# Scan tables of a hybrid decoder trunk: encoding table on GpSimd, direct table by one matmul a group

## Chip, core and metric

One core of a Trainium2 chip runs the whole program in one launch. The metric is device time in microseconds (us); lower is better. Engines are named as in the profile: PE (matmuls; PEld its weight loads), DVE (vector), ACT (scalar), POOL (GpSimd), SP (which here only issues DMAs).

## What is computed

The reference is a two-layer trunk over 256 positions of width 2048. Layer 0 runs a Mamba-2 scan and attention side by side; layer 1 is an S5 mixer: 128 groups of 16 channels, each driving a 64-dimensional diagonal complex state. Both layers end in a layer norm. The change is about small tables for layer 1 that depend on parameters alone and are made while layer 0 runs. Cut to what matters:

```python
def reference(x, ...):
    h = ssd_moba_mixer(x, ...)                 # layer 0
    x = layer_norm(ALPHA * x + h, ...)
    h = s5_mixer(x, ...)                       # layer 1
    return layer_norm(ALPHA * x + h, ...)

def s5_mixer(x, w_in, ...):
    u, gate = jnp.split(x @ w_in, 2, axis=-1)
    y = gelu(s5_ssm(u, ...))
    ga, gb = jnp.split(y @ w_glu, 2, axis=-1)
    return (ga * sigmoid(gb) * silu(gate)) @ w_out

def s5_ssm(u, ...):
    lam_bar = jnp.exp(lam * dt)                                 # per group, 64 complex
    b_bar = ((lam_bar - 1.0) / lam)[..., None] * (b_re + 1j * b_im)
    # h[t] = lam_bar * h[t-1] + b_bar @ u[t];  y[t] = Re(c @ h[t]) + d * u[t]
```

## The kernel before

**Big products.** Nearly all time is in products with weights in fp32, which are split in two parts: a weight unit of 128x1024 is loaded by SP into `raw` (L227), ACT copies it into `wh` in the reduced format fp32r (L230), DVE forms the rest `wl` (L232), and PE multiplies with both (L276, L282, L285). `raw`, `wh` and `wl` have four buffers each. A unit is 12 to 16 matmuls; PE goes through 433 units in a fixed order, and the splits are written three units ahead of their use (`split_to`).

**Small work between units.** Everything else is cut into jobs. After each unit `pump` runs one or more of `jobs` (due soon) and of `back` (spread evenly up to a goal). The framework then orders the instructions of each engine by a simulation of the time they take; `tc.issue_after(x)` keeps what stands under it behind x. At run time each engine, SP's and POOL's queues too, goes through its own list in that order and waits at the head of it for semaphores. A tile of a pool with `bufs=1` can be filled again only when all readers of its last content are done.

**Scan tables.** Layer 1 takes four positions at a time, so each of the 16 blocks of 8 groups needs in DRAM (`wb[b]`, 128x1792): an encoding table (512 columns, four inputs to the state), a decoding table (512), a direct table (256, inputs to outputs inside the four) and phasors (512). The jobs for a block are in `block_jobs` and `phasors`; block 0 begins near 390 us, they end near 790 us, and `ssm` of layer 1 loads `wb[b]` from 870 us on.
- `bars` loads `bc` on SP (L722) and weighs B; `efs` and `fcs` form the encoding table `et` and the decoding table `ob` on DVE (L748 to L762).
- `pes`, once for two blocks: eight transposes on PE turn `et` (L398), ACT copies them into `ob` (L772), which ACT stores; 16 matmuls of `et` with `cv` give the first column of the direct table (L779).
- `mts`: three matmuls with shift matrices (L789) give the other columns, three ACT copies place them (L793).
- `phasors`: on POOL alone, L698 to L711. Four sums of the rotary embedding (L938) in each of the four head groups of the attention stand on POOL as well.

Of the kernel before, what the change touches and what calls it, by code (L numbers as in the profile page):

```python
# [16 lines left out]
P = 128  # L17
# [19 lines left out]
SLOT = np.array([[8 * (q // 4) + 4 * (q % 2) + 2 * ((q // 2 % 2) ^ h) + q // 2 % 2 for q in range(64)] for h in range(2)])  # L37
GORDER = [16 * h + p + 8 * i for h in range(8) for p in range(8) for i in range(2)]
# [13 lines left out]
NCONST = _fields(CONST, [("ident", 128), ("causal", 256), ("tril", 128), ("shift", 384),  # L52
# [5 lines left out]
def _constants():  # L58
# [39 lines left out]
def _layout(inp):  # L98
# [66 lines left out]
def trunk(tc, io, out):  # L165
# [8 lines left out]
    with ExitStack() as top:  # L174
# [33 lines left out]
        keep = [None, range(0)]  # L208

        def split_to(i):  # L210
            while nsplit[0] <= min(i, len(units) - 1):
# [15 lines left out]
                nc.sync.dma_start(raw.rearrange("p k n -> p (k n)"), units[n])  # L227
# [185 lines left out]
        wb = [dram.tile([P, 1792], F32, name=f"wb{b}") for b in range(16)]  # L413
        rho = cst.tile([P, 64], F32, name="rho")
# [8 lines left out]
        with ExitStack() as l0:  # L423
# [168 lines left out]
            lap = pp.tile([P, 2, 64, 4], F32, name="lap")  # L592
# [5 lines left out]
            def trig_jobs():  # L598
# [38 lines left out]
            def table_jobs():  # L637
                em, ex, th, lr = dtl[:, 0:128], ta[:, 0, 0:128], ta[:, 1, 0:128], ta[:, 2, 0:128]
                sn, sh, co, t0 = (tb[:, i, 0:128] for i in range(4))
                re, im = nre[:, 0:128], nim[:, 0:128]  # L640
                li = sh
                wr, wi = wri[:, 0, :], wri[:, 1, :]
# [14 lines left out]
                def reals():  # L657
                    V.tensor_tensor(wr, em, re, op=OP.mult)
                    V.tensor_tensor(th, li, im, op=OP.mult)
                    V.tensor_tensor(wr, wr, th, op=OP.add)  # L660
                    V.tensor_tensor(wr, wr, t0, op=OP.mult)

                def imags():
                    V.tensor_tensor(wi, li, re, op=OP.mult)
                    V.tensor_tensor(th, em, im, op=OP.mult)
                    V.tensor_tensor(wi, wi, th, op=OP.subtract)
                    V.scalar_tensor_tensor(wi, wi, sgn, t0, op0=OP.mult, op1=OP.mult)
                    V.tensor_copy(lam[:, 0, :, 0], lr)
                    V.tensor_copy(lam[:, 1, :, 0], li)

                def power(w, n, k, a, b):
                    def go():
                        tp, tq = t0[:, 0:n], th[:, 0:n]
                        ar, ai = w[:, 0, :, a], w[:, 1, :, a]
                        br, bi = w[:, 0, :, b], w[:, 1, :, b]
                        V.tensor_tensor(tp, ar, br, op=OP.mult)
                        V.tensor_tensor(tq, ai, bi, op=OP.mult)
                        V.tensor_tensor(w[:, 0, :, k], tp, tq, op=OP.subtract)
                        V.tensor_tensor(tp, ar, bi, op=OP.mult)
                        V.tensor_tensor(tq, ai, br, op=OP.mult)  # L680
# [753 lines left out]
```

## Time and profile before

| | us |
|---|---|
| median of 3 runs (lowest, highest) | 1336.08 (1334.17, 1336.17) |
| profiled execution, its time | 1333.94 |
| its span (first to last instruction) | 1332.2 |
| PE busy, DVE busy, ACT busy, POOL busy | 1316.2, 1006.2, 697.2, 388.1 |
| mean granted clock of PE | 0.995 |

How to read the lines: a group's line names the line of the code, engine, operation, output<-inputs with shapes, count, then busy time and mean ns, then idle time of the engine before them and what ended it. A timeline line is start, length, engine, line, names, count. A line by stretch has for PE, PEld, DVE, ACT and POOL the busy us with the instruction count, then the granted clock (1.00 is full), the DMA engines' share and GB/s. A line of waits is: who waited <- for what, total us, times, longest. Records of an fp32 matmul come in two, so 16 matmuls are 32 records.

### The profile page before, as it was taken

What the parts mean: (1) busy time and instruction counts of PE and PEld (TensorE: products, weight loads), DVE (VectorE), ACT (ScalarE), POOL (GpSimd) and SP (SyncE); (2) the same over time, 40 slices, a digit from 0 to 9 for tenths busy, and PEclk for the clock granted to TensorE, in tenths of its full rate; (3) what the DMA queues carried; (4) which work ended last, traced back from release to release, by engine and by line L of the source; (5) the groups of instructions that cost most, each with busy time, mean ns of one, the idle gap of its engine ahead of it and who ended that gap; (6) DMA issues with size and microseconds to landing.
All of it is one profiled execution on the core that took longest, in us unless ns stands there. A gap on an engine that the chain in (4) does not pass through costs nothing.

```text
span 1332.2 us, 21933 instructions
## 1 busy us (share of the span) xinstructions
PE 1316.2 (99%) x8240; PEld 1115.5 (84%) x8240; DVE 1006.2 (76%) x1642; ACT 697.2 (52%) x952; POOL 388.1 (29%) x650
## 2 busy tenths in 40 slices
PE   9999999999999999999999999899999999999996
PEld 8888888878888888888888888888888888888885
DVE  5879847897798888889788766749899845555565
ACT  5667669964644544554653434334345544444441
POOL 0050000123028547738887400013343100000001
PEclk9999999999999999999999999999999999999998
DMA  8555565555546657556756668397988665555662
GB/s 314 193 172 181 190 251 195 171 171 176 174 158 238 208 187 249 202 190 221 262 193 227 235 235 309 121 311 254 307 288 311 208 218 189 187 192 187 253 211 81
DMA packets 81915, 287.04 MB, mean 215 GB/s; under 512 B 9984, under 2 KB 12672, under 8 KB 81296
## 3 DMA queue, kind: packets, MB, share of 16 engines
q1 hardware_dynamic: 69264, 243.51, 53.5%
q0 software_dynamic: 7360, 30.45, 6.8%
q10 hardware_dynamic: 5184, 11.67, 2.4%
q8 instruction: 65, 1.06, 0.3%
q14 instruction: 42, 0.34, 0.1%
HBM read 264.58 MB, written 21.00 MB: 214 GB/s over the span
## 4 chain that ended last, share of the span: by engine, by line
PE 98%; DVE 1%; ACT 0%; POOL 0%; issue 0%; POOLq 0%
PE main L276 46%; PE main L282 27%; PE main L285 14%; PE main L328 2%; PE aux L398 1%; PE aux L282 1%; PE aux L871 1%; PE aux L779 1%; PE enc L1223 1%; PE aux L409 1%; PE aux L285 1%; PE dec L1268 1%; PE aux L958 1%; PE aux L990 1%; PE dec L1264 0%; PE aux L789 0%
## 5 line engine op out<-in xcount | busy, mean ns | idle before, releaser
L232 DVE TENSOR_TENSOR wl<-raw,wh 128x1024 fp32r<-128x1024 f32 x431 | 536.6, 1248 | 276.3 <-ACT wh L230 271.1
L230 ACT ACTIVATE wh<-raw 128x1024 fp32r<-128x1024 f32 x431 | 455.3, 1059 | 525.7 <-PE main L276 268.5
L282 PE MATMUL main<-AB,wh 128*128 128x512 f32 x1344 | 479.1, 400 | 0.0
L285 PE MATMUL main<-AB,wl 128*128 128x256 f32 x1344 | 378.5, 282 | 0.0
L276 PE MATMUL main<-wh,AB 128*128 128x512 f32 x1024 | 322.1, 392 | 0.0
L282 PEld LDWEIGHTS main<-AB,wh 128*128 128x128 f32 x1344 | 252.4, 188 | 60.6 <-issue 1.8
L285 PEld LDWEIGHTS main<-AB,wl 128*128 128x128 f32 x1344 | 253.8, 189 | 1.5 <-issue 0.8
L276 PE MATMUL main<-wh,CF 128*128 128x512 f32 x768 | 241.2, 392 | 0.0
L276 PEld LDWEIGHTS main<-wh,AB 128*128 128x128 f32 x1024 | 192.0, 188 | 40.3 <-issue 0.6
L276 PE MATMUL main<-wl,AB 128*128 128x512 f32 x512 | 199.9, 390 | 0.0
L276 PEld LDWEIGHTS main<-wh,CF 128*128 128x128 f32 x768 | 144.0, 188 | 30.5
L276 PE MATMUL main<-wl,CF 128*128 128x512 f32 x384 | 149.8, 390 | 0.0
L706 POOL TENSOR_TENSOR c<-c 128x8 f32<-128x8 f32 (+2 forms) x192 | 105.7, 569 | 30.2 <-DMA wb<-c 22.6
L276 PEld LDWEIGHTS main<-wl,AB 128*128 128x128 f32 x512 | 96.2, 188 | 19.3
L276 PEld LDWEIGHTS main<-wl,CF 128*128 128x128 f32 x384 | 72.1, 188 | 14.7
L938 POOL TENSOR_TENSOR a<-a,b 64x512 f32<-64x512 f32 x16 | 34.7, 2171 | 145.8 <-DVE a L937 115.7
L880 POOL TENSOR_TENSOR ssq<-ssq,c 128x256 f32<-128x256 f32 x16 | 21.4, 1337 | 191.2 <-ACT c L878 190.6
L282 PE MATMUL main<-CF,wh 128*128 128x512 f32 x192 | 68.3, 399 | 0.0
L708 POOL TENSOR_TENSOR c<-c,c 128x4 f32<-128x4 f32 (+2 forms) x96 | 54.9, 572 | 7.5
L285 PE MATMUL main<-CF,wl 128*128 128x256 f32 x192 | 54.0, 281 | 0.0
L709 POOL TENSOR_TENSOR c<-c,c 128x4 f32<-128x4 f32 (+2 forms) x96 | 47.0, 489 | 0.0
L1379 POOL DMA_DIRECT2D AB<-in_lnr x1 | 0.6, 554 | 157.4 <-issue 157.4
(282 smaller groups left out, 1431.9 us busy)
## 6 DMA issues: line engine op xcount, KB each, us to landing
raw<-in_wi SPq DMA_DIRECT2D x271, 512.0 KB, 3.8
raw<-in_wo SPq DMA_DIRECT2D x96, 512.0 KB, 3.8
raw<-in_wglu SPq DMA_DIRECT2D x64, 512.0 KB, 3.3
wt<-wb POOLq DMA_DIRECT2D x16, 896.0 KB, 7.5
wb<-ob ACTq DMA_DIRECT2D x16, 512.0 KB, 5.4
bc<-in_s5bc SPq DMA_DIRECT2D x16, 256.0 KB, 3.3
a<-cumd SPq DMA_DIRECT2D x8, 512.0 KB, 6.6
wb<-c POOLq DMA_DIRECT2D x16, 256.0 KB, 3.2
```

The lines of the kernel that those rows point to most:

```text
L230: high = A.activation(wh, raw, AF.Copy)
L232: splits[n] = (high, V.tensor_tensor(wl, raw, wh.bitcast(F32), op=OP.subtract))
L276: T.matmul(ps[o], l[:, k, sl], r[:, j, :], start=start and i == 0, stop=stop and i == 2)
L282: T.matmul(ps[o].rearrange("p (a n) -> p a n", a=2), wh[:, j, sl], x2[:, :, k, :], start=start, stop=False, skip_group_check=True)
L285: T.matmul(ps[o][:, 0:S], wl[:, j, sl], x2[:, 0, k, :], start=False, stop=stop, skip_group_check=True)
L328: T.matmul(pv[o // 2][:, o % 2, :], l[:, j, sl], r[:, k, :], start=first and i == 0 and o % 2 == 0, stop=end and i == 2 and o % 2 == 1, sk ...
L398: end = T.transpose(dst[:, i * P : i * P + P], s, ident)
L706: G.tensor_tensor(p[:, :, :, 0:m], cs[:, :, :, 1 : m + 1], cs[:, i, :, n : n + 1].unsqueeze(1).to_broadcast([P, 2, 4, m]), op=OP.mult)
L708: G.tensor_tensor(cs[:, 0, :, n + 1 : n + 1 + m], p0[:, 0, :, 0:m], p1[:, 1, :, 0:m], op=OP.subtract)
L709: G.tensor_tensor(cs[:, 1, :, n + 1 : n + 1 + m], p0[:, 1, :, 0:m], p1[:, 0, :, 0:m], op=OP.add)
L880: G.tensor_tensor(ssq, ssq, jk[:, f, :], op=OP.add)
L938: turns.append(G.tensor_tensor(q[0:64], q[0:64], tm, op=OP.add))
```

## The change

1. The encoding table is made already turned, with the inputs on partitions, so that no transpose is needed. `loads` gets two more tiles per block on SP: `bt` (B, 128x512) and `lt` (two DMAs, weights times powers of lam_bar, from a DRAM tile `qd` that new table jobs `qpower` fill). `etable` makes the table with four operations on POOL and stores it from POOL; the decoding table is stored from ACT.
2. The decoding side `ft` is made on DVE in the layout of the direct table's operands (`fcs`), and `bb` repeats the weighed B four times (`wides`). `pes` then is one matmul with 64 moving columns for each of the 16 groups of two blocks, which gives all four columns of the direct table at once, unmasked.
3. `mts` places and masks them: one ACT copy with a mask as scale and three DVE operations on shifted views of PSUM, in place of the shift matmuls.
4. `loads` is kept behind the last `raw` load written so far, and `etable` behind the last rotary sum (`turns[-1]`), as `phasors` was. `bt`, `lt` and `te` have one buffer, `et`, `bb` and `ft` two.

```diff
-                nc.sync.dma_start(raw.rearrange("p k n -> p (k n)"), units[n])
+                lastraw[0] = nc.sync.dma_start(raw.rearrange("p k n -> p (k n)"), units[n])
...
+                def qpower(i):
+                    def go():
+                        times(q(i), [m[:, 128:192] for m in (wr, wi)] if i == 3 else q(i + 1), [m[:, 128:192] for m in (lr, li)], 64)
+                        if i % 2 == 0:
+                            nc.gpsimd.dma_start(qd[i : i + 2].rearrange("s p x -> p s x"), tb[:, i, :].rearrange("p (s x) -> p s x", s=2))
+                    return go
...
                 def bars():
+                    with tc.issue_after(lastraw[0].ins):
+                        loads()
+                    wides()
+
+                def loads():
                     bc = h["bc"] = pp.tile([P, 4, 8, 16], F32, tag="bc", name=nm("bc"))
                     nc.sync.dma_start(bc.rearrange("p a g m -> p (a g m)"), io["s5bc"][b].rearrange("p a g m -> p (a g m)"))
...
+                    bt = h["bt"] = pp.tile([P, 2, 4, 64], F32, tag="bt", name=nm("bt"))
+                    nc.sync.dma_start(bt.rearrange("p r a n -> p (r a n)"), io["s5bt"][b])
+                    lt = h["lt"] = pp.tile([P, 4, 2, 64], F32, tag="lt", name=nm("lt"))
+                    for i in range(2):
+                        src = qd[:, 64 * i + 4 * b : 64 * i + 4 * b + 4, :].rearrange("s a x -> s (a x)")
+                        nc.sync.dma_start(lt[64 * i : 64 * i + 64].rearrange("p a r n -> p (a r n)"),
+                                          src.unsqueeze(0).to_broadcast([16, 4, 512]))
+
+                def wides():
+                    bc = h["bc"]
+                    bb = h["bb"] = pp.tile([P, 8, 16, 4], F32, tag="bb", bufs=2, name=nm("bb"))
+                    tm = pp.tile([P, 2, 8, 16], F32, tag="tm", name=nm("tm"))
+                    wr, wi = (wri[:, i, gs].unsqueeze(2).to_broadcast([P, 8, 16]) for i in range(2))
+                    V.tensor_tensor(tm[:, 0], bc[:, 0], wr, op=OP.mult)
+                    V.tensor_tensor(tm[:, 1], bc[:, 1], wi, op=OP.mult)
+                    t0, t1 = (tm[:, i].unsqueeze(3).to_broadcast([P, 8, 16, 4]) for i in range(2))
+                    V.tensor_tensor(bb, t0, t1, op=OP.add)
 
                 def fcs():
                     bc = h["bc"]
...
+                    ft = h["ft"] = pp.tile([P, 8, 16, 4], F32, tag="ft", bufs=2, name=nm("ft"))
+                    tm = pp.tile([P, 8, 16, 3], F32, tag="tm", name=nm("tm"))
+                    lr, li = (lam[:, i, gs, :].unsqueeze(2).to_broadcast([P, 8, 16, 3]) for i in range(2))
+                    ca, cb = (bc[:, i].unsqueeze(3).to_broadcast([P, 8, 16, 3]) for i in (2, 3))
+                    V.tensor_copy(ft[:, :, :, 0], bc[:, 2])
+                    V.tensor_tensor(ft[:, :, :, 1:4], ca, lr, op=OP.mult)
+                    V.tensor_tensor(tm, cb, li, op=OP.mult)
+                    V.tensor_tensor(ft[:, :, :, 1:4], ft[:, :, :, 1:4], tm, op=OP.add)
+
+                def ets():
+                    with tc.issue_after(turns[-1].ins):
+                        etable()
+
+                def etable():
+                    bt, lt = h["bt"], h["lt"]
+                    et = pp.tile([P, 4, 2, 64], F32, tag="et", bufs=2, name=nm("et"))
+                    te = pp.tile([P, 4, 2, 64], F32, tag="te", name=nm("te"))
+                    for r, dst in enumerate((et, te)):
+                        G.tensor_tensor(dst, lt, bt[:, r].unsqueeze(2).to_broadcast([P, 4, 2, 64]), op=OP.mult)
+                    G.tensor_tensor(et[:, :, 0], et[:, :, 0], te[:, :, 1], op=OP.subtract)
+                    G.tensor_tensor(et[:, :, 1], et[:, :, 1], te[:, :, 0], op=OP.add)
+                    nc.gpsimd.dma_start(wb[b][:, 0:512], et.rearrange("p a r n -> p (a r n)"))
+                    fv = h["ft"].rearrange("p (h q) m t -> p h (q m t)", h=2)
                     for r in range(2):
...
+                        dst = wb[b][:, 512 + 256 * r : 768 + 256 * r].rearrange("(h n) x -> n h x", h=2)
+                        nc.scalar.dma_start(dst, fv[64 * r : 64 * r + 64])
 
                 def pes():
...
+                    pk = hk["pk"] = aux()
+                    for n, d in enumerate((pend.pop(), h)):
+                        for q in range(4):
+                            for at in range(2):
+                                i = q // 2
+                                a = 2 * (q % 2) + (i ^ at)
+                                T.matmul(pk[64 * at : 64 * at + 64, 256 * n + 64 * a : 256 * n + 64 * a + 64],
+                                         d["bb"][:, 4 * at + q].rearrange("p m s -> p (m s)"),
+                                         d["ft"][:, 4 * at + q].rearrange("p m t -> p (m t)"), start=True, stop=True)
+
+                def mts():
+                    pk = hk["pk"].rearrange("p (a m t) -> p a m t", m=16, t=4)
                     dc = PR("s5d")[:, 4 * b - 4 : 4 * b + 4].unsqueeze(2).to_broadcast([P, 8, 16])
...
+                    V.tensor_tensor(dd, C("kmask").unsqueeze(1).to_broadcast([P, 8, 16]), dc, op=OP.mult)
+                    V.tensor_tensor(pk[:, :, :, 0], pk[:, :, :, 0], dd, op=OP.add)
+                    sm = C("smask")
+                    A.activation(om.rearrange("p a m t -> p (a m t)"), hk["pk"], AF.Copy, scale=sm[:, 0:1])
+                    for t in range(1, 4):
+                        V.scalar_tensor_tensor(om[:, :, :, t:], pk[:, :, :, : 4 - t], sm[:, t : t + 1], om[:, :, :, t:],
+                                               op0=OP.mult, op1=OP.add)
```

The changed code moves lines: weight loads on SP are L225 (before L227), weight matmuls L274 (L276), the phasor work L709 to L722 (L698 to L711), the rotary sums L956 (L938).

On PE, at the first pair of blocks, before: transposes of the two blocks' `et`, the direct matmuls, and, 20 weight matmuls later, the shift matmuls.

```order
L276 MATMUL main_4081<-wh_4084,AB_75 128x512
L398 MATMUL aux_4184<-consts,et_3874 128x128 x4
L398 MATMUL aux_4191<-consts,et_4109 128x128 x4
L779 MATMUL aux_4182<-cv_3809,et_3874 64x16 x8
L779 MATMUL aux_4182<-cv_4071,et_4109 64x16 x8
L276 MATMUL main_4080<-wh_4121,AB_75 128x512
...
L789 MATMUL aux_4252<-kt_4183,consts 128x128 x3
```

At the same place after:

```order
L274 MATMUL main_4092<-wh_4043,AB_75 128x512
L792 MATMUL aux_4147<-ft_3827,bb_3800 64x64 x8
L792 MATMUL aux_4147<-ft_4063,bb_4036 64x64 x8
L274 MATMUL main_4091<-wh_4071,AB_75 128x512
L274 MATMUL main_4091<-wl_4073,AB_75 128x512
```

Transposes and shifts are gone, and 16 matmuls of 64 columns stand where 16 of 16 columns stood.

On SP, at block 13 before: among the weight loads `raw` stands one load of `bc`.

```order
L227 DMA raw_7569<-in_wo 128x1024
L227 DMA raw_7599<-in_wo 128x1024
L722 DMA bc_7587<-in_s5bc 128x512
L227 DMA raw_7617<-in_wo 128x1024
L227 DMA raw_7645<-in_wo 128x1024
```

At block 13 after:

```order
L225 DMA raw_7350<-in_wo 128x1024
L225 DMA raw_7400<-in_wo 128x1024
L737 DMA bc_7418<-in_s5bc 128x512
L739 DMA bt_7420<-in_s5bt 128x512
L743 DMA lt_7422<-qd 64x1x512 x2
L225 DMA raw_7430<-in_wo 128x1024
L225 DMA raw_7454<-in_wo 128x1024
```

Behind `bc` stand the loads of `bt` and `lt`, and the next weight loads stand behind them; in the list of waits `bt` waits for POOL. This place is two weight loads earlier in the list than before.

On POOL, before, from the end of block 12's phasors (`wb_88` is block 12's part of DRAM, `wb_89` block 13's): nothing but phasors.

```order
L711 DMA wb_88<-c_1197_7519 128x512
L698 MEMSET c_1245_7807 128x4
L699 MEMSET c_1245_7807 128x4
L701 COPY c_1245_7807<-phi 128x4 x2
L706 TENSOR_TENSOR c_1246_7808<-c_1245_7807 128x8
```

After, block 12's encoding work (`et_7305`, which reads block 12's `bt_7226` and `lt_7228`) inside the phasors of block 13:

```order
L722 DMA wb_88<-c_1179_7368 128x512
L709 MEMSET c_1224_7634 128x4
...
L719 TENSOR_TENSOR c_1224_7634<-c_1225_7635,c_1226_7636 128x4x4
L776 TENSOR_TENSOR et_7305<-lt_7228,bt_7226 128x512
L776 TENSOR_TENSOR te_7306<-lt_7228,bt_7226 128x512
L720 TENSOR_TENSOR c_1224_7634<-c_1225_7635,c_1226_7636 128x4x4
L777 TENSOR_TENSOR et_7305<-et_7305,te_7306 128x4x64
L778 TENSOR_TENSOR et_7305<-et_7305,te_7306 128x4x64
...
L779 DMA wb_88<-et_7305 128x512
```

After the last rotary sum POOL's list is: phasors of block 8 (encoding of 9 inside), of 9, of 10 (encoding of 10 inside), of 11 (11 inside), of 12, of 13 (12 inside), of 14, of 15 (13 inside), then the encoding of 14 and 15. So the phasors, which wait for no load, run up to two blocks ahead of the encoding work, which waits for SP's loads.

More of the change, by code (lines that the diff above doesn't have):

```diff
@@ L37 @@
 SLOT = np.array([[8 * (q // 4) + 4 * (q % 2) + 2 * ((q // 2 % 2) ^ h) + q // 2 % 2 for q in range(64)] for h in range(2)])
+DUP = np.concatenate([SLOT[:, 4 * b : 4 * b + 4].reshape(-1) for b in range(16)])
 GORDER = [16 * h + p + 8 * i for h in range(8) for p in range(8) for i in range(2)]
@@ L671, in power @@
-                def power(w, n, k, a, b):
-                    def go():
[L673 to L680, printed above, removed]
-                        V.tensor_tensor(w[:, 1, :, k], tp, tq, op=OP.add)
-                    return go
@@ L684, in table_jobs, with weights @@
-                return [parts, norms, reals, imags] + [power(w, n, k, a, b) for w, n, top in ((lam, 128, 3), (lap, 64, 4))
-                                                       for k, a, b in ((1, 0, 0), (2, 1, 0), (3, 1, 1)) if k < top]
+                    V.tensor_tensor(ex, ex, th, op=OP.add)
+                    V.tensor_tensor(th, li, re, op=OP.mult)
+                    V.tensor_tensor(em, em, im, op=OP.mult)
+                def weights():
+                    V.tensor_tensor(th, th, em, op=OP.subtract)
+                    V.tensor_tensor(wr, ex, t0, op=OP.mult)
+                    V.tensor_tensor(wi, th, t0, op=OP.mult)
+                    V.tensor_scalar(wri[:, 0, :], wr[:, 0:128], nsg, None, op0=OP.mult)
+                    V.tensor_scalar(wri[:, 1, :], wi[:, 0:128], -1.0, None, op0=OP.mult)
+                    V.tensor_copy(lam[:, 0, :, 0], lr[:, 0:128])
+                    V.tensor_copy(lam[:, 1, :, 0], li[:, 0:128])
@@ new lines, in times, with power @@
+                def times(out, a, b, n):
+                    tp, tq = t0[:, 0:n], th[:, 0:n]
+                    V.tensor_tensor(tp, a[0], b[0], op=OP.mult)
+                    V.tensor_tensor(tq, a[1], b[1], op=OP.mult)
+                    V.tensor_tensor(out[0], tp, tq, op=OP.subtract)
+                    V.tensor_tensor(tp, a[0], b[1], op=OP.mult)
+                    V.tensor_tensor(tq, a[1], b[0], op=OP.mult)
+                    V.tensor_tensor(out[1], tp, tq, op=OP.add)
+                def power(k, a, b):
+                    def go():
+                        times(*([lam[:, i, :, n] for i in range(2)] for n in (k, a, b)), 128)
+                    return go
@@ new lines, in signed, with q @@
+                def signed():
+                    V.tensor_scalar(lam[:, 1], lam[:, 1], sgn, None, op0=OP.mult)
+                def q(i):
+                    return [tb[:, 2 * (i // 2), 128 * (i % 2) + 64 * r : 128 * (i % 2) + 64 * r + 64] for r in range(2)]
+                def qpower(i):
[4 more added lines that the diff above has]
+                    return go
@@ L687, in trunk @@
+                return [parts, norms, parts2, weights, power(1, 0, 0), power(2, 1, 0), signed] + [qpower(i) for i in (3, 2, 1, 0)]
             turns = []
```

134 lines of the change are left out of this document (32 added, 102 removed).

## The prediction

> **What bounds the kernel now.** I read the page's busy row and chain first, then busy time by stretch, then PE's timeline in the stage that the change touches, last the queues of POOL and SP there.
>
> ```profile
> span 1332.2 us, 21933 instructions
> PE 1316.2 (99%) x8240; PEld 1115.5 (84%) x8240; DVE 1006.2 (76%) x1642; ACT 697.2 (52%) x952; POOL 388.1 (29%) x650
> ...
> PE 98%; DVE 1%; ACT 0%; POOL 0%; issue 0%; POOLq 0%
> ```
>
> PE is busy for 99% of the span and is 98% of the chain. So an instruction less on PE is time won, as long as its weights keep coming. The stage with the tables (about 385 to 790 us) in its last third, and the one place where PE stood still:
>
> ```profile
> 617.00:757.00 140.00, 140.00 (x762) 117.73 (x761) 112.66 (x216) 69.56 (x97) 112.74 (x233) 1.00 0.68 232
> 840.00:860.00 20.00, 16.47 (x134) 15.45 (x132) 15.14 (x26) 5.54 (x10) 0.00 (x0) 0.91 0.15 53
> L232 DVE TENSOR_TENSOR wl<-raw,wh 128x1024 fp32r<-128x1024 f32 x45 | 56.8, 1266 | 26.6 <-ACT wh L230 26.4
> L232 DVE TENSOR_TENSOR wl<-raw,wh 128x1024 fp32r<-128x1024 f32 x65 | 79.7, 1226 | 79.6 <-ACT wh L230 78.9
> ```
>
> From 617 to 757 us PE never waits, while DVE (112.7 of 140, 80%) and POOL (112.7) are also nearly full. The third row is DVE's weight split in that stretch, the fourth the same from 1100 to 1280 us, where POOL is idle.
>
> **PE's part of the change.**
>
> ```profile
> 411.88 0.39 PE L276 MATMUL main<-wl,AB 128*128 128x512 f32 x1
> 412.11 0.39 PE L276 MATMUL main<-wh,AB 128*128 128x512 f32 x1
> 412.34 1.03 PE L398 MATMUL aux<-consts,et 128*128 128x128 f32 x8
> 413.30 1.11 PE L779 MATMUL aux<-cv,et 128*64 128x16 f32 x32
> 414.34 0.50 PE L276 MATMUL main<-wh,AB 128*128 128x512 f32 x1
> 414.68 0.39 PE L276 MATMUL main<-wl,AB 128*128 128x512 f32 x1
> ...
> 419.93 0.83 PE L789 MATMUL aux<-kt,consts 128*128 128x128 f32 x6
> 420.51 0.48 PE L276 MATMUL main<-wh,AB 128*128 128x512 f32 x1
> ...
> 226.90 1.52 PE L871 MATMUL aux<-b,CF 128*64 128x256 f32 x16
> 228.35 0.50 PE L282 MATMUL main<-AB,wh 128*128 128x512 f32 x1
> ```
>
> Starts count, not durations: weight matmuls start 0.23 us apart. Transposes and direct matmuls hold PE from 412.34 to 414.34, and the matmul behind them takes 0.34 instead of 0.23: 2.11 us. The shifts hold it for 0.58 (419.93 to 420.51) and about 0.1 behind: 0.68. A pair of blocks costs 2.79, eight pairs 22.3 us.
>
> After, a pair costs 32 records of 128 rows by 64 weight columns and 64 moving columns. From below, L779 has the same weight loads and 16 moving columns: 413.30 to 414.34, 1.04 us. The moving columns are priced by L871, also in two column halves: 16 records, eight with 256 and eight with 128 columns, 3072 in all, take 1.45 us, 0.47 ns a column; 2048 columns are 0.97 us. L871 loads its weights underneath, so I take the larger, 1.04, and 0.11 behind it: 1.15. From above the two add up: 2.12. PE's gain is 1.64 a pair (at least 0.67), **13.1 us** over eight pairs (at least 5.4).
>
> **DVE, ACT, DMA.** From 617 to 757 us:
>
> ```profile
> L748 DVE TENSOR_TENSOR et<-bb,lam 128x128 f32<-128x128 f32 x18 | 7.3, 440 | 0.0
> L749 DVE TENSOR_TENSOR tm<-bb,lam 128x128 f32<-128x128 f32 x18 | 7.1, 433 | 0.0
> L762 DVE TENSOR_TENSOR ob<-ob,tm 128x256 f32<-128x256 f32 x10 | 4.6, 460 | 0.2
> L735 DVE TENSOR_SCALAR cv<-bc,consts 128x128 f32<-128x128 f32 x6 | 3.2, 534 | 0.0
> L750 DVE TENSOR_TENSOR et<-et,tm 128x384 f32<-128x384 f32 x5 | 3.1, 611 | 0.0
> ```
>
> A block today: six strided products at 0.44, six of 128x256 at 0.46, one 128x384 at 0.61, eight small ones near 0.4 and half of a pair's three: some 9.8 us. After: three of 128x384 at 0.61, one 128x512 near 0.7, three small ones, half of a pair's five: 4.9. That takes 4.9 of a block's 26 us (below) off DVE: 80% becomes some 62%. ACT makes one copy a pair instead of five. The table jobs grow by nine operations and by half in width near 100 to 160 us, where PE never waits either. I cost all of this at nothing on PE's path: the cover is the splits' lead over PE (worked out below), and if that were gone, splits would come late there. The new loads bring 512 KB a block to SP's queue, one weight unit more in some eight, with DMA at 0.68.
>
> **POOL's and SP's part.** Call the phasor work of a block P (L698 to L711) and the new encoding work E: two multiplies of 128x512, two sums of 128x256, a DMA issue.
>
> ```profile
> 613.49 4.27 POOL L938 TENSOR_TENSOR a<-a,b 64x512 f32<-64x512 f32 x1 [4.33 <-DVE a L937]
> ...
> L722 SPq DMA_DIRECT2D bc<-in_s5bc x15: 327/328/382, 394.9 to 763.7; - x15
> ...
> L698 POOL MEMSET c<- x8: 124/126/182, 617.7 to 738.4; 128x4 f32 x8
> ...
> L711 POOL DMA_DIRECT2D wb<-c x8: 587/587/627, 635.0 to 756.4; - x8
> ...
>   POOL c L706: 17.3, 7
> ...
> L938 POOL TENSOR_TENSOR a<-a,b x16: 1263/1781/6302, 274.3 to 613.5; 64x512 f32<-64x512 f32 x16
> ...
> L880 POOL TENSOR_TENSOR ssq<-ssq,c x16: 733/1193/4335, 223.9 to 322.9; 128x256 f32<-128x256 f32 x16
> ```
>
> A block has 26.3 us (SP's loads of bc: 368.8 over 14). After the last rope sum (613.5) eight P run back to back from 617.7 to 757.0: 17.4 us each, 2.5 of it waiting for its own store (17.3 over 7). POOL is slower the busier DVE is: the same L938 takes 1263 to 1781 ns at the median. With DVE at 62% I take P = 15.7, a tenth off, nearer to the upper row because the splits stay; bounds 17.4 (no relief) and 13.1 (14.9 x 1263/1781 + 2.5: as if no DVE were beside it). E: multiply 1.9 (1.26 to 2.2), sum 1.1 (0.73 to 1.3), issue 0.59: **6.6 us** (4.6 to 7.6).
>
> Nobody on PE waits for P. E is different: the tiles bt and lt have one buffer, so SP may issue block b+1's load of bt only when E of block b has multiplied, and weight loads stand behind it on SP. The order above puts E of block 12 behind P of blocks 8 to 12 and 0.4 of 13, and E of block 13 another 2.2 P later.
>
> ```profile
> SPq L227 <- DVE wl L232: 235.5, 89, 5.8
> ACT wh L230 <- PE main L276: 268.5, 167, 3.3
> ...
> 700.82 12.71 SPq L227 DMA_DIRECT2D raw<-in_wo  x5
> 713.75 0.33 SPq L722 DMA_DIRECT2D bc<-in_s5bc  x1
> 715.58 16.88 SPq L227 DMA_DIRECT2D raw<-in_wo  x7
> 733.15 0.33 SPq L722 DMA_DIRECT2D bc<-in_s5bc  x1
> 735.17 2.41 SPq L227 DMA_DIRECT2D raw<-in_wo  x2
> ...
> L230 ACT ACTIVATE wh<-raw 128x1024 fp32r<-128x1024 f32 x431 | 455.3, 1059 | 525.7 <-PE main L276 268.5
> ...
> raw<-in_wo SPq DMA_DIRECT2D x96, 512.0 KB, 3.8
> ```
>
> SP waits in its own order today too (first row), and ACT's split waits for PE to free a buffer (second), so there is slack. With four buffers of raw, wh and wl and 12 matmuls x 0.23 = 2.72 us a unit: PE ends unit k at 0, unit k+4 is split at 2.4 (1.06 on ACT, 1.27 on DVE), raw k+8 is issued, lands at 6.2 and must be split by 19.0 (seven units), so landed by 16.6. **SP may be late by 10.4 us**; beyond that PE stands.
>
> Block 13's bt stands two loads before its bc of today (713.75), near 707; six of the eight pairs lie before it and have saved 9.8: 697. E12 has multiplied at 609 (last rope sum, four pairs earlier) + 5.4 x 15.7 + 3 x 6.6 + 2 x 1.9 = 717. SP is blocked for 20 us, 10 beyond its slack. In those, splits starve, DVE is idle and POOL near its fast rate (1263/1781, x 0.7): a stall of 7, E12 at 714. E13: 714 + 2.8 + 2.2 x 15.7 + 3.8 = 755; SP gets to block 14's bt near 735 - 9.8 + 7 = 732. Blocked for 23, beyond by 12.6, x 0.7: a stall of 9. Together **16 us**. PE's clock also falls: in 840 to 860 us, after 3.5 us of idle or small matmuls, the granted clock is 0.91, 1.8 us lost, so twice 1.7: **3.4**.
>
> [...]
>
> Sum: 1333.9 (span 1332.2, 1.7 around it) - 13.1 + 16 + 3.4 = 1340; the median of the runs shown, 1336.08, is 2.1 above its profiled run, so I say 1342 for a median.
>
> **Rivals.** (1) *Faster*: E comes in time and PE keeps its 13.1: 1321, some 1323 for a median. For it: no PE wait in 617 to 757 today, and P and E together (22.3) are less than a block's 26.3 us. Against: P runs ahead of E in POOL's order. With P = 13.1 and E = 4.6, E12 multiplies at 609 + 71 + 14 + 2.5 = 696 and nothing stalls. It decides near P = 14.5: there the stalls (2 and 7) and the clock (3.4) eat the gain, and there is *no change*. (2) *Worse*: P stays at 17.4, E costs 7.6. E12 multiplies at 730, E13 at 770: stalls of some 18 and 14, 1358 for a median; blocks 11 and 12 may then stall too. (3) POOL's longer operations hold up DVE's splits. The rows say little: L232 takes 1266 ns beside a full POOL, 1226 beside an idle one, 40 ns x 45, under DVE's waits of 26.6. Even 1.26 us for each of E's four operations is 5 us in 26, and DVE has 38% to spare: 1321, as rival 1. (4) *The change gives PE little*: the new records take twice as long, 2.12 a pair; L871 speaks against it. Without stalls 1328, with them 1348.
>
> [...]
>
> **How the numbers follow.** The stalls have chance 0.55, rival 1 0.28 (rival 3 in it), near cancellation 0.1, rival 2 0.07 (rival 4 lies inside these). The likeliest case's own range is 1337 to 1354. From rival 1's 1320 to rival 2's 1360 holds eight in ten. A measurement tells 0.2% (2.7 us) from no change. Faster: rival 1 and a little of the stalls' lower tail, 0.31; same 0.11; slower 0.58.
>
> **What would show it.** Right: PE with 256 records of the new matmul at about 33 ns a start and no L398 on et; SP waiting for POOL's multiply for 15 to 30 us at the bt loads of blocks 13 and 14 (700 to 760 us); PE waits there of 7 to 10 us each, with ACT's split waiting for raw; granted clock under 1 behind them. Wrong: P under 14 us, or SP waits under 10 us, with PE full to 800 us (then 1321); or PE waits before 690 us (then rival 2). A new matmul at 60 ns a start would halve PE's gain.

## The result and the profile after

The changed kernel takes 1354.58 us in the median of four runs (1352.5 to 1357.04), beside 1335.39 for the kernel before on the same chip: ratio 1.0149, interval 1.0137 to 1.0161. The forecast was 1342, 6 us slower; it is 19 us slower. The profiled execution of the changed kernel took 1357.04 us, 2.5 above its median.

From the page: span, busy time, the granted clock in 40 slices, and the chain.

```profile
span 1354.9 us, 21669 instructions
PE 1315.5 (97%) x8128; PEld 1108.4 (82%) x8128; DVE 1001.0 (74%) x1441; ACT 685.5 (51%) x920; POOL 462.5 (34%) x732
...
PEclk9999999999999999999997999999999999999999
...
PE 74%; POOL 14%; DVE 5%; DMA 3%; issue 2%; ACT 1%; SPq 0%; POOLq 0%; ACTq 0%; DVEq 0%
```

PE was 98% of the chain and is 74% now; POOL has come in with 14%. PE's busy time has not fallen although it has 112 matmul records less; in e2 below, the same change without its stalls, it is 1304.8. Most of the difference is matmuls at half clock: after the first stall weight matmuls start 0.43 us apart in place of 0.23. What PE waited for (us in all, times, longest):

```profile
PE main L274 <- ACT wh L228: 13.8, 2, 10.6
PE main L274 <- DVE wl L230: 4.0, 3, 2.0
PE main L283 <- DVE wl L230: 3.3, 3, 1.9
```

What SP waited for from 400 to 800 us, in the same form:

```profile
SPq L225 <- DVE wl L230: 162.8, 76, 5.2
SPq L739 <- POOL te L776: 64.4, 7, 14.3
...
SPq L739 <- POOL c L720: 17.3, 1, 17.3
...
SPq L739 <- POOL c L717: 9.9, 1, 9.9
```

L739 is the load of `bt`. SP stands there for POOL, 92 us in nine waits; before, it never waited for POOL at its table loads. The last three rows belong together: what frees bt is the second multiply of E (the encoding work of a block on POOL, as in the prediction), and the rows that name `c` put the wait down to phasor work of the same moment. SP's timeline at the worst place:

```profile
712.21 0.42 SPq L737 DMA_DIRECT2D bc<-in_s5bc  x1
729.85 0.33 SPq L739 DMA_DIRECT2D bt<-in_s5bt  x1
730.28 1.16 SPq L743 DMA_DIRECT2D lt<-qd  x2
731.53 19.69 SPq L225 DMA_DIRECT2D raw<-in_wo  x10
...
766.11 0.33 SPq L739 DMA_DIRECT2D bt<-in_s5bt  x1
```

And POOL's:

```profile
727.34 1.27 POOL L776 TENSOR_TENSOR et<-lt,bt 128x512 f32<-128x512 f32 x1
728.56 1.26 POOL L776 TENSOR_TENSOR te<-lt,bt 128x512 f32<-128x512 f32 x1
```

SP is ready for block 13's bt at 712.6, POOL finishes multiplying for block 12 at 729.8, SP issues bt's load at 729.85 and only then, behind lt's, the next weights. For those 17 us SP stands, and no weight load is issued. The stretches of PE around it (PE, PEld, DVE, ACT, POOL; then clock, DMA share, GB/s):

```profile
717.00:727.60 10.60, 10.60 (x47) 8.47 (x46) 3.82 (x5) 0.88 (x1) 8.51 (x23) 1.00 0.07 25
727.60:731.00 3.40, 0.05 (x1) 0.00 (x0) 0.00 (x0) 0.00 (x0) 3.40 (x5) 1.00 0.09 7
731.00:734.40 3.40, 0.00 (x0) 0.00 (x0) 0.00 (x0) 0.00 (x0) 3.22 (x10) 0.50 0.79 148
734.40:737.80 3.40, 0.00 (x0) 0.00 (x0) 0.00 (x0) 0.70 (x1) 2.95 (x10) 0.50 0.98 374
737.80:741.20 3.40, 2.53 (x5) 1.73 (x6) 2.98 (x6) 2.32 (x3) 0.29 (x2) 0.50 0.97 395
741.20:744.60 3.40, 3.40 (x10) 2.17 (x11) 3.19 (x3) 1.21 (x2) 2.36 (x3) 0.50 0.95 284
744.60:748.00 3.40, 3.40 (x37) 2.92 (x38) 1.42 (x2) 1.06 (x1) 3.01 (x10) 1.00 0.75 273
```

The DMA engines run dry first (a share of 0.07), PE lives on its buffers until 727.7 and stands for 10.6 us. From its restart at 738.2 it works another 6.4 us at half clock.

**Where the time goes, by one ruler.** Both kernels run the same 5888 weight matmuls in the same order. The table gives, for each profiled execution, how much later (plus) than in the kernel before the n-th of them starts; e1 to e9 are the experiments below. This is the ruler that the text means from here on.

| n | before, us | after | e1 | e2 | e3 | e4 | e5 | e6 | e7 | e8 | e9 |
|---|---|---|---|---|---|---|---|---|---|---|---|
| 1 | 9.1 | 0.6 | 0.7 | -0.4 | 0.5 | 0.4 | 0.0 | 0.3 | 0.3 | 0.5 | -0.7 |
| 2101 | 423.4 | -1.6 | -1.5 | -2.6 | -1.7 | -1.8 | -2.3 | -0.8 | -1.9 | -1.7 | -2.7 |
| 3001 | 609.6 | -0.4 | -6.0 | -6.5 | -6.1 | -0.5 | -6.7 | -4.9 | -5.7 | -3.4 | -6.3 |
| 3451 | 717.7 | 1.1 | -3.9 | -8.7 | -7.7 | 1.9 | -8.7 | -2.8 | -7.3 | 5.5 | -6.3 |
| 3601 | 754.5 | 13.8 | -5.5 | -10.2 | -9.2 | 0.4 | -10.3 | -4.4 | -9.1 | 9.8 | 1.2 |
| 3901 | 825.5 | 20.8 | 5.0 | -11.9 | -10.9 | -1.2 | -2.8 | 7.6 | -10.7 | 15.4 | -0.4 |
| 5888 | 1320.7 | 22.7 | 7.8 | -10.9 | -9.7 | 1.5 | -0.4 | 9.9 | -6.2 | 17.6 | -0.8 |

Before 423 and after 890 us nothing of the 22.7 arises but 0.6 at the start. Small losses have eaten a gain of 9 by 717 us; then come two jumps.

### The profile page after: what moved, and what is told of

Same layout as the page of the kernel before. It is cut to its first block, busy times and chain, and to the rows that moved or that the text cites. A ratio compares the mean times of both kernels' runs of the same rounds, so it can differ in the third digit from the quotient of the medians.

```text
span 1354.9 us, 21669 instructions
## 1 busy us (share of the span) xinstructions
PE 1315.5 (97%) x8128; PEld 1108.4 (82%) x8128; DVE 1001.0 (74%) x1441; ACT 685.5 (51%) x920; POOL 462.5 (34%) x732
## 4 chain that ended last, share of the span: by engine, by line
PE 74%; POOL 14%; DVE 5%; DMA 3%; issue 2%; ACT 1%; SPq 0%; POOLq 0%; ACTq 0%; DVEq 0%
PE main L274 35%; PE main L280 20%; PE main L283 10%; POOL c L717 5%; POOL c L719 3%; DVE wl L230 2%; POOL c L720 2%; PE main L326 2%; DMA wb<-c 2%; DMA raw<-in_wi 1%; PE aux L280 1%; POOL te L776 1%; PE aux L889 1%; POOL et L776 1%; POOL et L778 1%
## 5 line engine op out<-in xcount | busy, mean ns | idle before, releaser
L230 DVE TENSOR_TENSOR wl<-raw,wh 128x1024 fp32r<-128x1024 f32 x431 | 554.3, 1293 | 301.0 <-ACT wh L228 297.7
L274 PE MATMUL main<-wh,AB 128*128 128x512 f32 x1024 | 324.1, 394 | 10.6 <-ACT wh L228 10.6
L274 PE MATMUL main<-wh,CF 128*128 128x512 f32 x768 | 243.1, 394 | 3.3 <-ACT wh L228 3.3
L274 PEld LDWEIGHTS main<-wh,AB 128*128 128x128 f32 x1024 | 193.1, 189 | 51.7 <-ACT wh L228 11.0
L274 PE MATMUL main<-wl,AB 128*128 128x512 f32 x512 | 201.3, 393 | 2.1 <-DVE wl L230 2.0
L274 PEld LDWEIGHTS main<-wh,CF 128*128 128x128 f32 x768 | 145.4, 190 | 34.5 <-ACT wh L228 3.7
L274 PE MATMUL main<-wl,CF 128*128 128x512 f32 x384 | 150.8, 393 | 2.0 <-DVE wl L230 2.0
L274 PEld LDWEIGHTS main<-wl,AB 128*128 128x128 f32 x512 | 96.7, 189 | 23.1 <-DVE wl L230 3.6
L274 PEld LDWEIGHTS main<-wl,CF 128*128 128x128 f32 x384 | 72.8, 190 | 17.3 <-DVE wl L230 2.3
L956 POOL TENSOR_TENSOR a<-a,b 64x512 f32<-64x512 f32 x16 | 28.6, 1788 | 98.3 <-DVE a L955 93.1
L719 POOL TENSOR_TENSOR c<-c,c 128x4 f32<-128x4 f32 (+2 forms) x96 | 50.0, 521 | 6.9
L280 PEld LDWEIGHTS main<-CF,wh 128*128 128x128 f32 x192 | 36.0, 188 | 8.7
```

The costliest lines, as they stand in the source:

```text
L230: splits[n] = (high, V.tensor_tensor(wl, raw, wh.bitcast(F32), op=OP.subtract))
L274: T.matmul(ps[o], l[:, k, sl], r[:, j, :], start=start and i == 0, stop=stop and i == 2)
L280: T.matmul(ps[o].rearrange("p (a n) -> p a n", a=2), wh[:, j, sl], x2[:, :, k, :], start=start, stop=False, skip_group_check=True)
L719: G.tensor_tensor(cs[:, 0, :, n + 1 : n + 1 + m], p0[:, 0, :, 0:m], p1[:, 1, :, 0:m], op=OP.subtract)
L956: turns.append(G.tensor_tensor(q[0:64], q[0:64], tm, op=OP.add))
```

## The experiments

The theory: E stands behind phasors on POOL (P is the phasor job of a block) and bt has one buffer, so SP stands at bt with the weight loads behind it. PE runs out of weights and then works at half clock. Rival A: the extra loads make the weights late. Rival B: POOL's long operations hold up DVE's splits. Each run was taken beside the kernel before on its own chip; the ratios are to that.

**e1: two buffers for bt and lt.**

```diff
-tag="bt", name=...    -tag="lt", name=...    -tag="et", bufs=2, name=...
+tag="bt", bufs=2, ... +tag="lt", bufs=2, ... +tag="et", name=...
```

> The changed kernel with two buffers each for bt and lt (and one for et, to make room). The work, the traffic and the order of POOL stay; only SP's wait at the load of bt moves a block later. Theory (POOL's encoding comes late behind phasors, SP waits at bt with the weight loads behind it, PE starves and its clock halves): SP's waits at bt fall from 91 us in all to under 15, PE's idle gaps from 420 to 780 us from 23.4 us to under 4, time 1318 to 1326. Rival A (the new loads and the DMA traffic make the weights late): gaps stay at 15 to 23 us, time 1345 to 1355. Rival B (POOL's long operations hold up DVE's splits): the same 1345 to 1355.

Measured: 1342.66 us, ratio 1.0066 (1.0050 to 1.0082). The time lies between the theory's range and the rivals'. All PE gaps of the changed kernel before 750 us but one are gone, the small ones at 436 and 540 to 573 us too, with traffic as it was; that speaks against A. But one wait of SP at bt is left, and it is as long as the earlier ones:

```profile
SPq L739 <- POOL te L776: 16.0, 1, 16.0
```

What PE waited for:

```profile
PE main L274 <- ACT wh L228: 7.1, 2, 5.9
...
PE aux L792 <- DVE ft L765: 2.1, 1, 2.1
```

E of block 13 still multiplies at 765.4 us, behind the phasors of all blocks up to 14 and part of 15, and now block 15's bt waits for it, to 767.9. The buffer moved the wait, it did not shorten POOL's queue.

The gap that stays is 2.1 us long, at 618 us. There PE waits for DVE's `ft`, as it did for 1.2 us at 624 in the changed kernel, but here SP has not waited at bt. DVE at this place:

```profile
614.15 3.24 DVE L763 TENSOR_TENSOR ft<-bc,lam 128x384 f32<-128x384 f32 x1
```

And POOL:

```profile
614.43 1.29 POOL L776 TENSOR_TENSOR te<-lt,bt 128x512 f32<-128x512 f32 x1
615.68 1.28 POOL L776 TENSOR_TENSOR et<-lt,bt 128x512 f32<-128x512 f32 x1
```

The same DVE operation takes 0.54 us at its fastest in the changed kernel; here it ends only when both of POOL's multiplies are done. Behind the gap PE works 3.4 us at half clock. That fits rival B, at this one place; e8 and e9 have such a gap too (1.3 and 1.7 us).

**e2: no encoding work.** The loads of bt and lt and E are left out.

```diff
-bt = ...; nc.sync.dma_start(bt...)   # and lt, and the four operations G.tensor_tensor
-nc.gpsimd.dma_start(wb[b][:, 0:512], et...)
+nc.scalar.dma_start(wb[b][:, 0:512], h["ft"]...)
```

> The changed kernel without the encoding table: no loads of bt and lt, no work for it on POOL; its columns are filled with a copy of the decoding table. What is left is the change on PE, DVE and ACT. Both the theory and the rivals A and B expect no gaps of PE before 800 us; the run prices PE's gain by itself: 1336 - 13 = 1323 if the prediction's 1.64 us a pair holds (1321 to 1325), 1326 to 1330 if a pair saves half of it.

Measured: 1324.65, ratio 0.9929 (0.9912 to 0.9945), within 1321 to 1325. No PE gap from 50 to 830 us, as expected. The table has the gain grow steadily from -0.4 to -11.9 at 825 us: 11.5, or 1.44 a pair, where 1.64 was forecast.

**e3: light phasors.**

```diff
-G.memset(...); G.tensor_copy(...); while n < 64: ...   # all of the phasor work
+G.memset(cs.rearrange("p a q c -> p (a q c)"), 1.0)
```

> The changed kernel with the phasor work of each block left out but for one fill of the tile and its store (the phasors are wrong values); encoding work, loads, buffers and DVE's work stay. Theory (the backlog of phasors ahead of the encoding work is what makes SP wait): SP's waits at bt under 20 us in all, gaps under 4 us, time 1318 to 1326. Rival A (traffic): 1345 to 1355. Rival B (POOL's long operations, the multiplies of 128x512, hold up the splits): at least half of the loss stays, 1338 or more.

The phasor work is left out but for one fill and the store, so the phasors are not computed; the run serves for its time alone. Measured: 1324.6, ratio 0.9930 (0.9916 to 0.9945), PE gaps 0.33 us before 830 us. From 400 to 800 us SP's waits at bt are down from 92 us:

```profile
SPq L727 <- POOL te L764: 5.8, 3, 3.0
```

With all of E, the loads and the single buffers in place, next to nothing is lost once the phasors are away. A falls here: the loads of bt and lt are all there. B falls in the form that E's operations alone would cost time.

**e4: phasors behind the encoding work.**

```diff
 with tc.issue_after(turns[-1].ins):
-    phasors(b)
+    with tc.issue_after(etd[b].ins):   # the last operation of E of block b
+        phasors(b)
```

> The changed kernel with one tie more: the phasors of a block stand behind the encoding work of the same block on POOL. All work and traffic stay, buffers too. Theory: encoding of blocks 12 and 13 comes one phasor job (17 us) earlier, about 710 and 745 us, SP's waits at their successors' bt fall from 17.1 and 14.3 us to under 6, the two large stalls (16.3 us with 6.7 us of half clock) go, smaller ones may stay: 1325 to 1334. Rivals A and B: the order does not matter, 1350 to 1356.

Measured: 1337.13, ratio 1.0026 (1.0010 to 1.0043), above the range by 3. The two large stalls are gone (E of block 12 multiplied at 708.5, of block 13 at 728.7). The smaller waits at bt of blocks 2, 6, 9 and 11 stay (9.5, 9.1, 14.4, 11.2 us), and with them gaps of 5.9 us and two periods at half clock. The order of the jobs alone is worth 16 of the 19 us.

**e5: both cures.** e1 and e4 together.

> Both cures together: two buffers for bt and lt (one for et), and the phasors of a block behind the encoding work of the same block. Theory (every lost microsecond is a PE gap from SP waiting at bt, or the half clock behind it): no wait of SP at bt over 6 us, PE gaps from 420 to 780 us under 3 us, no half clock there, 1322 to 1328, as the runs without encoding work (1324.65) and with light phasors (1324.6). Rival (POOL's long operations beside DVE's splits: in the run without encoding work the mean split from 617 to 705 us took 1249 ns, in the changed kernel 1424): the splits stay at 1390 or more and starve PE at other places, 1333 to 1340.

Measured: 1332.58, ratio 0.9991 (0.9982 to 1.0). A miss, and a useful one. No wait at bt, no gap before 790 us, as the theory has it, but then one of 5.8 us. PE's longest wait:

```profile
PE main L274 <- ACT wh L228: 5.7, 1, 5.7
```

SP's new wait:

```profile
SPq L1102 <- DMA wb<-c: 12.3, 1, 12.3
```

And the timelines of SP and, after it, of POOL there:

```profile
791.53 0.80 SPq L1102 DMA_DIRECT2D row<-in_lnr  x2
```

```profile
788.93 0.59 POOL L724 DMA_DIRECT2D wb<-c  x1 [0.30 <-POOL c L722]
```

L1102 loads the rows of the first layer norm into space that the tables held; SP must wait until the last phasors are stored, and POOL issues that store at 788.9 only. Weights stand behind SP again. So POOL is late as a whole, not just in the order of its jobs. The time comes within 0.4 us of the rival's range, but not in the rival's way: no gap stands in the stretch with the slow splits.

**e6: loads of bt and lt on POOL's queue.**

```diff
-nc.sync.dma_start(bt...)      -nc.sync.dma_start(lt[64 * i : ...
+nc.gpsimd.dma_start(bt...)    +nc.gpsimd.dma_start(lt[64 * i : ...
```

> The changed kernel with the loads of bt and lt issued by POOL's queue instead of SP's; one buffer each as before. POOL's order changes with it: the encoding work of blocks 10 to 15 now stands ahead of their phasors. SP no longer waits for POOL at all. Theory: no PE gaps over 0.5 us from 420 to 780 us, 1322 to 1328, though POOL waits some 3 us a block for its own loads. Rival (contention of POOL with DVE's splits): 1333 to 1345, with gaps that end at the splits wl.

Measured: 1344.35, ratio 1.0083 (1.0060 to 1.0106). A miss. The order changes with it (all encoding work now stands ahead of the phasors of block 10), SP never waits at bt, and the same end as in e5 comes later still: SP waits 17.3 us for the last phasor store, PE stands 9.8 us at 802 us, and 1.9 us at 668. The time lies in the rival's range, but the long gap ends with ACT's split behind SP's late load, not with the splits `wl`. The wait can be moved along POOL's queue, and each time the weights pay.

**e7: the encoding work on DVE.**

```diff
-with tc.issue_after(turns[-1].ins):
-    etable()
+etable()
-G.tensor_tensor(...)   # four operations
+V.tensor_tensor(...)
-nc.gpsimd.dma_start(wb[b][:, 0:512], et...)
+nc.scalar.dma_start(wb[b][:, 0:512], et...)
```

> The changed kernel with the four encoding operations of a block on DVE instead of POOL (the store on ACT's queue, no tie to the rotary sum). POOL then has the phasors alone, as in the kernel before; buffers, loads and traffic are those of the changed kernel. Theory: bt is free as soon as DVE has multiplied, no wait of SP at bt for POOL, 1322 to 1328; DVE gets some 2.5 us a block more but its splits go back to 1250 to 1300 ns. Rival (DVE's load near 80% is what matters): PE gaps of 10 us or more, 1335 to 1350.

Measured: 1324.8, ratio 0.9934 (0.9920 to 0.9948), with all the work done: this version is faster than both kernels. PE has no gap between 50 and 830 us. SP waits at bt for DVE, 2.0 us at most:

```profile
SPq L739 <- DVE te L775: 4.1, 5, 2.0
```

The edit also drops the tie of E to the rotary sum; e8 does that alone. DVE takes E in 2.6 us a block:

```profile
L775 DVE TENSOR_TENSOR te<-lt,bt 128x512 f32<-128x512 f32 x15 | 11.8, 784 | 0.0
L775 DVE TENSOR_TENSOR et<-lt,bt 128x512 f32<-128x512 f32 x15 | 11.4, 763 | 0.0
L777 DVE TENSOR_TENSOR et<-et,te 128x256 f32<-128x256 f32 x15 | 8.1, 538 | 0.0
L776 DVE TENSOR_TENSOR et<-et,te 128x256 f32<-128x256 f32 x15 | 7.4, 494 | 0.2
```

**e8: no tie of the encoding work to the rotary sum.**

```diff
-with tc.issue_after(turns[-1].ins):
-    etable()
+etable()
```

> The changed kernel without the tie of the encoding work to the last rotary sum; all else stays. On POOL the encoding work of blocks 0, 4, 5, 8 and 9 moves ahead of a rotary sum or of phasors; blocks 10 to 15 keep their places. Theory: the waits of SP at bt for blocks 6 and 9 (9.1 and 12.2 us) shrink and the small PE gaps with them (7.2 us in all in the changed kernel, 4 to 7 of them gone), the two large stalls at 727 and 770 us stay: 1346 to 1352. If the tie matters for the large stalls too: 1325 to 1335. If ties cost nothing: 1353 to 1357.

Measured: 1354.12, ratio 1.0153 (1.0134 to 1.0171), no different from the changed kernel, as if ties cost nothing (1353 to 1357); above the theory's range by 2. SP's waits at bt fall from 92 to 61 us and the gaps from 23.5 to 18.3, but the wait at block 11 grows from 11.5 to 18.6 us and the large stalls are spread over 669, 732 and 766 us. The tie alone is not what costs.

**e9: a dose, shorter phasors.**

```diff
-while n < 64:
-    m = min(n, 63 - n)
+G.memset(cs[:, :, :, 33:64], 1.0)
+while n < 32:
+    m = n
```

> A dose: the changed kernel with the last doubling step of each phasor job left out (its half of the columns is filled with one value, so the phasors are wrong there): four of the longest operations, about 3.3 us of some 17 in the changed kernel's trace, so P near 13.5 to 14.5. Encoding work of block 12 stands one phasor job later in POOL's order than in the changed kernel, the rest as it was. The prediction's rule (break-even near P = 14.5, nothing stalls at 13.1): 1322 to 1336. Theory by the changed kernel's own trace: encoding of block 12 multiplied near 718 us where SP comes for its successor's bt near 705, so a wait of 13 and a stall of 3 to 5 us, and a smaller one at 750; the small stalls before 630 us mostly stay: 1332 to 1344. Rival (P has no part in it): 1352 to 1357.

Measured: 1338.74, ratio 1.0041 (1.0027 to 1.0055), inside the theory's range. Half of each block's phasors is a fill here, so this run too serves for its time alone. The profiled execution was the fastest of its five (1333.58), which is why the table ends at -0.8; where the others lost 5 us more is not known. In it SP waits 12.2 us at block 13's bt and PE stands 5.8 us at 720: with P near 13 us in place of 17.1 the first stall is about half and the second gone. Yet with phasor jobs of 13.0 and 13.4 us just ahead of it (starts at 684.0, 697.0, 710.4) the gain was still eaten. E of block 12 stands one such job later than in the changed kernel, so this does not fix the break-even, but 14.5 was too high by the order that the chip ran here.

## Why the prediction was wrong in size

The sign, the engine, the queue and the place were right: SP at the loads of bt for blocks 13 and 14, 17.3 and 14.3 us (forecast 20 and 23), E of block 12 multiplied at 730 (forecast 714 to 717), of block 13 at 766 (755), PE stalls there. Four terms were off. Against e2, which is the change without its stalls, the changed kernel loses 33.6 us in the ruler above (22.7 + 10.9). By steps:

| step | forecast | measured in the profiled execution | shown by |
|---|---|---|---|
| PE's gain | -13.1 | -11.5 at 825 us, -10.9 at the end | e2 |
| two large stalls | +16 | 11.0 + 5.3 = +16.3 | gaps at 727.7 and 739.0; 770.3 and 774.0 |
| half clock behind them | +3.4 | 3.2 + 3.4 = +6.6 | ruler less gaps |
| small stalls before 690 us | 0 | +8.7, of which gaps 7.2 | gone in e5, and in e1 but for the one at 618 us |
| start, and the transition to layer 1 at 860 us | 0 | 1.0 + 0.9 = +1.9 | ruler |
| sum | +6.3 | +22.6 (ruler 22.7) | |

**The term that failed** is "a stall of 7 ... a stall of 9", as the list of *all* stalls. I took one slack of 10.4 us for every block and looked for longer waits from block 12 on only. SP waited 9.5, 9.1 and 12.2 us at bt of blocks 2, 6 and 9 already, and behind them PE stood 1.9, 1.4 and 2.7. (Of the 2.7, 1.2 are the wait for DVE's `ft`; the gap of 1.1 at 573 us is a wait for `b` of the attention on DVE.) So 8.7 us stand where the sum had nothing.

The slack is not one figure. Waits of 11.5, 9.9 and 11.2 us (changed kernel, blocks 11 and 12; e4, block 11) cost nothing. At block 13 a wait of 17.3 cost 11.0, and in e9 one of 12.2 cost 6.2; at block 11 of e8 one of 18.6 cost only 6.4. A wait less the stall behind it thus lies between 6 and 12 us. In each of these cases SP had issued four weight loads more than DVE had split when it began to wait, so all four buffers of `raw` were taken; what else makes the difference is open.

That the two large stalls came out right in sum is luck. By the prediction's own rule (what is beyond 10.4 us, times 0.7) the measured waits would have cost 4.8 and 2.7 us, not 11.0 and 5.3; the forecast had longer waits and a kinder slack. SP and POOL were both late there. PE's gain was gone by then, so SP reached bt 15 to 20 us later than forecast. E of block 12 had multiplied at 729.8 in place of 717, and nearly all of that delay was there at the last rotary sum already: it ended at 621.1, where the forecast has 609, and from there POOL took 108.7 us (forecast 108). In e2, without E, it ended at 606.8, and in e1, with E but without the small stalls ahead of it, at 614.1. So of these 14 us about half goes with E of block 8, which POOL does just ahead of the last rotary sum, and half with the small stalls.

The text named PE waits before 690 us as the sign of its rival 2. That rival's mechanism came in (P of 17.1, E of block 12 done at 730, of block 13 at 766, 1354.6 us beside its 1358), though its stalls of 18 and 14 did not.

**P, and why DVE was not relieved.** DVE, forecast at 62%, stood at 81% in 617 to 705 us. The same stretch by engine, before:

```profile
617.00:705.00 88.00, 88.00 (x500) 74.61 (x499) 72.66 (x148) 48.73 (x74) 74.47 (x151) 1.00 0.69 234
```

after:

```profile
617.00:705.00 88.00, 85.17 (x467) 70.65 (x466) 71.19 (x99) 46.49 (x66) 73.81 (x133) 1.00 0.75 257
```

and in e2:

```profile
617.00:705.00 88.00, 88.00 (x487) 73.79 (x486) 63.17 (x104) 47.65 (x67) 74.79 (x152) 1.00 0.69 229
```

DVE has 49 instructions less and is nearly as busy. Without E it does fall, to 72%: that is 9.5 us in 88, some 2.8 a block of 26.3 us, where the prediction had 4.9. So E on POOL goes with 8.0 us more of DVE's time in this stretch, for 99 instructions in place of 104. Of these, 3.2 are DVE's own splits, which take longer. They are, in the same stretch, before:

```profile
L232 DVE TENSOR_TENSOR wl<-raw,wh 128x1024 fp32r<-128x1024 f32 x28 | 34.5, 1238 | 14.8 <-ACT wh L230 14.6
```

after:

```profile
L230 DVE TENSOR_TENSOR wl<-raw,wh 128x1024 fp32r<-128x1024 f32 x28 | 39.3, 1424 | 13.0 <-ACT wh L228 13.0
```

e2, with phasors alone on POOL:

```profile
L230 DVE TENSOR_TENSOR wl<-raw,wh 128x1024 fp32r<-128x1024 f32 x29 | 36.1, 1249 | 20.4 <-ACT wh L228 20.4
```

e3, with the encoding alone:

```profile
L230 DVE TENSOR_TENSOR wl<-raw,wh 128x1024 fp32r<-128x1024 f32 x31 | 40.5, 1317 | 13.0 <-ACT wh L228 13.0
```

e5:

```profile
L230 DVE TENSOR_TENSOR wl<-raw,wh 128x1024 fp32r<-128x1024 f32 x31 | 45.2, 1476 | 11.2 <-ACT wh L228 11.1
```

e7, where the encoding is on DVE itself:

```profile
L230 DVE TENSOR_TENSOR wl<-raw,wh 128x1024 fp32r<-128x1024 f32 x28 | 36.3, 1295 | 14.2 <-ACT wh L228 14.2
```

With E on POOL each split is longer than before by 79 ns (e3) to 238 ns (e5). With phasors alone on POOL it is longer by 11 in e2 and by 57 in e7, so of the 79 not all need be E's. That POOL's work is what lengthens them is the author's reading of these differences and of the long `ft` operation of e1; how the one engine holds up the other is not shown. From 400 to 790 us ten DVE instructions of the changed kernel take over 2.2 us (up to 5.1), none in the kernel before, one each in e2 and e7. The prediction's 1.26 us for each of E's four operations would have been 5 us a block; the splits show 5 us in these 88 (28 x 186 ns), some 3.3 blocks.

To cost this at nothing on PE's path was nearly right. e5 has the longest of these splits and no gap before 790 us; but in e1 PE did stand 2.1 us at 618 for a DVE operation of 3.24 us that ended only behind POOL's multiplies.

The relief of P failed by itself. Beside a busy DVE single operations of POOL are longer: in the kernel before the phasors' step of 128x248 (L706, 32 times) takes 0.62 us in the mean of the eight that DVE accompanies for less than 0.4 of their length, 1.03 in the mean of the 21 with more than 0.8. But in e2, with DVE down to 72% and phasors alone on POOL, seven jobs from 606.7 to 724.8 take 16.9 us each, where the kernel before has 17.2 (617.7 to 738.4) and the prediction took 15.7. No run shows DVE at 62%. In the changed kernel four phasor jobs and three of E (17.9 us between them) take the 86.2 us from 621.1 to 707.3, so P is 17.1. E was priced from the rows of 617 to 757 us a little high: 1.28 + 1.78 for the multiplies, 0.80 + 1.31 for the sums, 0.58 for the issue, 5.8 measured against 6.6. What the longer P cost up to block 12's E, the shorter E and an earlier place of it in the phasors of block 13 (4.2 us in, 6.3 forecast) gave back, which is why POOL's 108.7 us came out as forecast.

**PE's gain.** A group of the new matmuls with no weight matmul in between:

```profile
406.64 0.39 PE L274 MATMUL main<-wh,AB 128*128 128x512 f32 x1
406.96 1.15 PE L792 MATMUL aux<-ft,bb 128*64 128x64 f32 x32
408.04 0.50 PE L274 MATMUL main<-wh,AB 128*128 128x512 f32 x1
408.37 0.39 PE L274 MATMUL main<-wl,AB 128*128 128x512 f32 x1
```

From 406.64 to 408.04 are 1.40 us, less the 0.23 of a weight matmul 1.17, and 0.10 behind it: 1.27 against 1.15; the 0.09 ahead of the group was missed. 2.79 - 1.27 is 1.52, near the 1.44 of e2. The lower of the two bounds was the right choice.

**The clock.** The prediction took 1.7 us for each stall, which is what the one period at half clock that the kernel before has ahead of its end costs (3.413 us from 845.6). In the changed kernel it is at half from 731.0 to 744.6 (6.4 us of PE's work after the restart, rows above) and for 6.8 us from 775.3. In each case the first 3.4 us in which PE was back (busy for 2.5 from 737.8, 2.8 from 775.3) did not lift it.

## What to carry to other kernels

Where a queue in order carries the weights, any load with one buffer that is put on it ties the weights to the last reader of that buffer (here nine waits of SP, 92 us); cost it by the reader's place in its own engine's order, block by block from the first, not only where the backlog is largest. A second buffer or another queue moves such a wait along while the reading engine is late as a whole (16.0 us in e1, 17.3 in e6); here it ended only when work left that engine (e7, 9 us faster than before; e3, without the phasors). And a relief that one engine is to get from work moved to its neighbour is to be checked in the neighbour's presence: here DVE lost 49 instructions and hardly any time (72.7 to 71.2 us of 88).

## What was not expected of the hardware

The half-clock periods of these traces lie on a grid. In the changed kernel they begin at 731.0, 775.3, 867.5 and 877.7 us, which is 13, 40 and 43 times 3.413 us apart from the first, and they last four, two, one and one times 3.413; in the kernel before the one at 845.6 lasts 3.413, and the one at the program's end, from 1323.5, begins 140 times 3.413 behind it. What a gap cost in clock went with where it fell. In e4 a gap of 2.07 us lies in one period of the grid, the next is at half; in the changed kernel gaps of 1.16 and 1.57 fall into two neighbouring ones, and the clock stays. Two periods of e4:

```profile
436.90:440.30 3.40, 1.33 (x8) 0.93 (x8) 3.40 (x3) 1.30 (x2) 3.40 (x4) 1.00 0.38 83
440.30:443.70 3.40, 3.40 (x12) 2.86 (x11) 3.40 (x4) 1.25 (x3) 3.38 (x4) 0.50 0.80 198
```

And three of the changed kernel:

```profile
621.80:625.20 3.40, 2.24 (x36) 1.64 (x36) 3.40 (x2) 2.12 (x2) 3.40 (x5) 1.00 0.96 369
625.20:628.60 3.40, 1.83 (x15) 1.28 (x11) 3.40 (x3) 2.12 (x2) 3.40 (x5) 1.00 0.67 208
628.60:632.00 3.40, 3.40 (x19) 2.90 (x18) 2.73 (x4) 0.53 (x1) 3.14 (x8) 1.00 0.89 257
```

How much idle time in a period of the grid lowers the clock is not settled by these runs. The next period was at half behind 2.07 us (e4, from 436.9), 1.75 (e1, from 618.4), 1.54 and 1.52 (changed kernel, from 864.1 and 874.3), but not behind 1.57 and 1.68 (changed kernel, from 625.2 and 768.5). So idle time as the records have it does not decide alone, and what else counts is open. Once at half, the clock stayed there for another period behind 0.87 and 0.66 us of idle (changed kernel, from 737.8 and 775.3), and came back behind 0.38 (from 877.7) and 0.25 (kernel before, from 845.6). That is how the large stalls came to cost 3.2 and 3.4 us of clock and not 1.7. At the transition to layer 1, where both kernels have gaps of 0.3 to 1.3 us, there is one half period in the kernel before and there are two in the changed kernel.
